# A gated-recurrence stage with one table for tanh and silu, an undecayed state, an out-projection over four heads and ScalarE work ordered by table set

## The chip, the cores and the metric

The kernel runs on the 8 NeuronCores of one Trainium2 chip, as two dies of four cores (0 to 3 and 4 to 7). Each core computes 2 of the 16 sequences and exchanges nothing with the others. The metric is the device time of the slowest core, in microseconds (us), as a median of runs. PE is the TensorE matmul engine, ACT is ScalarE, DVE is VectorE, POOL is GpSimd; PSUM is the memory that matmuls accumulate in.

Some runs here were in a slower state: one die (at times both) was granted a lower TensorE clock (0.927 against 0.975 in the profile of the four heads alone, below). Where stages are compared, I use a core whose die was undisturbed, and say which.

## The reference, cut to what matters

Two layers, each with a half-step SwiGLU FFN, a token mixer, cross-attention to 256 memory tokens and a second FFN. The mixer of layer 0 is HGRN2, a gated linear recurrence with 8 heads of 128 channels; that of layer 1 is a convolution module. D is 1024, 2048 tokens a sequence.

```python
def hgrn2_mixer(h, w_in, head_norm, w_out, lb):
    q, f, i, g = jnp.split(h @ w_in, 4, axis=-1)
    q = jax.nn.silu(q)
    log_forget = jnp.log(lb + (1.0 - lb) * jax.nn.sigmoid(f))
    k = (1.0 - lb) * jax.nn.sigmoid(-f)
    v = i
    # by chunks: G = cumsum(log_forget); o = (q exp(G)) @ state + masked scores @ v
    # new_state = state * exp(G_last) + (k exp(G_last - G))^T v
    ...
    o = rms_norm(o, head_norm)            # per head
    o = o * jax.nn.silu(g)
    return o @ w_out
```

## The kernel before: the parts that the change touches

All work is recorded as operations with their reads and writes. A list scheduler on the host then orders each engine's operations with assumed durations, and the engines run these fixed orders, with semaphores between them. So any edit gives a new order everywhere.

An HGRN stage has 32 *units* for each sequence: one head and 512 tokens. The unit's core, cut:

```python
bf, bq, bgt = grp(1), grp(0), grp(3)      # f, q, g: 8 matmuls of 128x512 each
act: A = Sigmoid(bf);  SQ = Sigmoid(bq);  SG = Sigmoid(bgt)
act: Bf = Ln(A * (1-lb) + lb)             # log of the forget gate
dve: SQ = bq * SQ;  gs = bgt * SG         # the two silus
pool: A = (1-lb) * (1 - A)                # k
dve: Cf = scan(rmask, Bf)                 # G, cumulated over 128 tokens
act: Bf = Exp(Cf);  Cf = Exp(-Cf)
pool: qg = SQ * Bf;  kg = A * Cf
...                                       # v projection (32 small matmuls), scores, k transposed
# state, four chunks of 128 tokens; e = Bf's last column of the chunk
for c in range(4):
    dve: dSe[c] = ds_psum[c] * e[c]
for c in range(4):
    dve: stF[c] = stF[c-1] * e[c] + dSe[c]        # float32 for the next step
    dve: stB[c] = stF[c-1] * e[c] + dSe[c]        # the same again in bf16, for the matmul
...                                       # o, its per-head norm with Ln and Exp
dve: og = o_psum * rsB;  ogT = og * head_norm * gs
# out-projection, for every head: 8 matmuls with a contraction of 128, 8 additions
for t4 in range(4):
    for half in range(2):
        pe: b = ogT[:, t4] @ w_out[head][:, half]
        dve: h[tt, half] += b
```

Elsewhere, norms take Sqrt on ACT and a reciprocal on DVE. The softmax denominators and the layer norm of the convolution stage take DVE reciprocals of 128x512. ACT takes its functions from table sets. Where an operation needs another set than the one before it, a table load stands in the trace (1.28 us each, 346 of them on core 4 before); the tool chain put it in wherever the order of ACT's operations asked for one.

The softmax here doesn't subtract the row's maximum and nothing guards it: scores larger than these inputs give would overflow.

## Time and profile before

The median was 6838.54 us in 3 runs (6781.57 to 7608.12). This is the view of the cores: span and mean granted clock.

```profile
core 0: 6843.2 us, clock 0.957
core 4: 6774.9 us, clock 0.966
die 0 (median of its cores): 6807.1 us, clock 0.963
die 1 (median of its cores): 6775.6 us, clock 0.966
```

Core 0 spent 314 us at 13/16 of the clock and core 4 none. I read core 4 from here on.

The windows view of core 4 before. Columns: stretch and its length, then for PE, weight loads, DVE, ACT and POOL the busy time (instructions), then granted clock, DMA share and GB/s. The rows are the first HGRN stage, the attention stage after it, the conv stage and the attention stage after that, each from its first matmul to that of the next stage.

```profile
571.00:1105.00 534.00, 386.24 (x2776) 214.87 (x2773) 415.45 (x839) 358.32 (x461) 133.40 (x127) 0.91 0.18 20
1105.00:1296.00 191.00, 171.42 (x899) 80.27 (x900) 144.89 (x174) 82.86 (x136) 12.17 (x14) 0.97 0.40 54
2253.00:2738.00 485.00, 420.96 (x1939) 186.91 (x1937) 335.16 (x270) 127.14 (x201) 209.18 (x67) 0.93 0.15 22
2738.00:2912.00 174.00, 158.34 (x842) 75.48 (x842) 115.13 (x115) 63.60 (x102) 5.98 (x7) 0.98 0.28 42
```

The groups of DVE in the HGRN window (busy us, mean ns of one, then idle time before and its releaser) show the additions to h and the doubled state update:

```profile
L555 DVE TENSOR_TENSOR h<-ps,h 128x512 f32<-128x512 f32 x232 | 143.0, 676 | 0.6 <-PE ps L1021 0.6
L988 DVE SCALAR_TENSOR_TENSOR arena<-arena 128x128 f32<-128x128 f32 x112 | 38.8, 347 | 0.0
L990 DVE SCALAR_TENSOR_TENSOR arena<-arena 128x128 bf16<-128x128 f32 x112 | 38.5, 344 | 0.0
```

The timeline of ACT on core 4 before, one unit of the steady part (start us, length us, instruction, idle time before and releaser):

```profile
873.53 1.28 ACT L930 ACT_TABLE_LOAD   x1 [0.93 <-DVE arena L990]
874.83 0.81 ACT L930 ACTIVATE arena<-arena,vecs 128x512 f32<-128x512 f32 x1
...
880.31 1.28 ACT L928 ACT_TABLE_LOAD   x1 [2.09 <-PE ps L921]
881.60 0.60 ACT L928 ACTIVATE arena<-ps 128x512 f32<-128x512 f32 x1
882.21 1.28 ACT L1005 ACT_TABLE_LOAD   x1
883.51 0.60 ACT L1005 ACTIVATE arena<-ps 128x512 f32<-128x512 f32 x1
884.20 0.63 ACT L1006 ACTIVATE arena<-arena 128x512 f32<-128x512 f32 x1
884.85 1.28 ACT L929 ACT_TABLE_LOAD   x1
```

Four loads stand in one unit: the order goes from Ln and Exp to one sigmoid, back for the per-head norm's Ln and Exp, and to a sigmoid again. The waits of PE in the same HGRN window (us in total, times, longest us) name both the DVE additions and ACT:

```profile
PE ps L1021 <- DVE h L555: 36.0, 41, 1.3
PE ps L943 <- ACT arena L1005: 33.1, 20, 1.7
PE ps L980 <- ACT arena L975: 30.5, 24, 5.9
```

### The profile page before, as it was taken

To read this page: it belongs to the slowest core of one execution; us is meant where nothing else is said; L and a number is where in the kernel's file an instruction comes from. 1 tells how busy PE (TensorE), PEld (TensorE's weight loads), DVE (VectorE), ACT (ScalarE), POOL (GpSimd) and SP (SyncE) were. 2 spreads that over 40 slices of the span, in tenths; PEclk is the share of its full clock that TensorE was granted. 3 is DMA by queue.
4 is the path that set the end of the run, shared out by engine and by line. 5 is a ranking of instruction groups with operands and counts; after the bars stand their busy time and mean duration, and the time that the engine had idled before them with its cause. 6 is when DMAs were issued, how large, how long until landed. Compare 5 with 4: busy or idle time off the path is not lost.

```text
span 6843.2 us, 92702 instructions; the slowest of 8 cores (6762.6 to 6843.2 us)
## 1 busy us (share of the span) xinstructions
PE 6095.5 (89%) x30572; PEld 2877.5 (42%) x31144; DVE 4501.0 (66%) x6622; ACT 1990.2 (29%) x2973; POOL 952.1 (14%) x717
## 2 busy tenths in 40 slices
PE   4998767999999987999889986689999999878998
PEld 2444334444444433444334443344444444334443
DVE  3658777756665487665656687776665563876656
ACT  2116665311311322311221266642112122223212
POOL 0002221000000453000000022200000004530000
PEclk9999999999999998999989989999998998989999
DMA  5222113322221201232432212134333312013221
GB/s 106 38 33 29 18 18 54 45 40 38 41 38 19 35 1 26 43 50 38 96 74 38 30 21 21 15 50 56 38 38 38 38 13 34 1 27 42 41 38 59
DMA packets 367914, 258.86 MB, mean 38 GB/s; under 512 B 114241, under 2 KB 331329, under 8 KB 367456
## 3 DMA queue, kind: packets, MB, share of 16 engines
q0 software_dynamic: 346560, 205.55, 23.6%
q1 hardware_dynamic: 20896, 47.35, 2.3%
q8 instruction: 270, 4.42, 0.3%
q14 instruction: 188, 1.54, 0.1%
HBM read 441.61 MB, written 16.78 MB: 67 GB/s over the span
## 4 chain that ended last, share of the span: by engine, by line
PE 76%; DVE 10%; issue 6%; ACT 5%; DMA 2%; SPq 1%; POOL 0%; DVEq 0%; ACTq 0%; POOLq 0%
PE ps L591 36%; PE ps L606 17%; PE ps L843 4%; PE ps L789 4%; PE ps L692 3%; PE ps L921 3%; PE ps L679 3%; PE ps L807 2%; PE ps L524 1%; DVE h L555 1%; DMA arena<-xattn_wkv 1%; DVE arena L819 1%; ACT L1005 1%; DVE arena L827 1%; SPq L470 1%
## 5 line engine op out<-in xcount | busy, mean ns | idle before, releaser
L591 PE MATMUL ps<-arena 128*128 128x512 bf16 x11037 | 2503.8, 382 | 21.9 <-ACT arena L593 7.8
L608 DVE SCALAR_TENSOR_TENSOR h<-ps,h 128x512 f32<-128x512 f32 x2816 | 1730.3, 682 | 7.6 <-PE ps L606 5.9
L591 PEld LDWEIGHTS ps<-arena 128*128 128x128 bf16 x11264 | 1105.2, 98 | 1347.3 <-issue 81.1
L594 DVE TENSOR_TENSOR arena<-ps,arena 128x512 bf16<-128x512 f32 x704 | 485.9, 691 | 1363.3 <-PE ps L591 1334.2
L606 PE MATMUL ps<-arena 128*128 128x512 bf16 x5505 | 1281.4, 382 | 16.1 <-DVE h L608 7.8
L593 ACT ACTIVATE arena<-ps 128x512 bf16<-128x512 f32 x704 | 419.9, 597 | 2970.7 <-PE ps L591 2963.2
L606 PEld LDWEIGHTS ps<-arena 128*128 128x128 bf16 x5632 | 551.0, 98 | 681.8 <-issue 51.7
L555 DVE TENSOR_TENSOR h<-ps,h 128x512 f32<-128x512 f32 x704 | 447.3, 682 | 159.4 <-PE ps L692 103.9
L552 POOL DMA_DIRECT2D arena<-ffn_w_in x176 | 156.5, 891 | 2593.2 <-PE ps L591 2004.3
L843 PE MATMUL ps<-arena 128*128 128x512 bf16 x1942 | 466.6, 397 | 46.4 <-DVE arena L819 30.7
L921 PE MATMUL ps<-arena 128*128 128x512 bf16 x1478 | 382.3, 406 | 14.2 <-ACT arena L975 4.0
L496 ACT ACTIVATE junk<-h 128x1024 bf16<-128x1024 f32 x288 | 302.1, 1050 | 300.6 <-DVE h L555 185.4
L817 POOL TENSOR_TENSOR arena<-identf,dwT 128x2688 bf16<-128x2688 f32 x64 | 315.0, 4923 | 370.7 <-PE ps L843 278.5
L520 DVE SCALAR_TENSOR_TENSOR hn_tok<-h,stat,gB 128x1024 bf16<-128x1024 f32 x256 | 322.4, 1276 | 41.4 <-PE ps L524 27.6
L843 PEld LDWEIGHTS ps<-arena 128*128 128x128 bf16 x1984 | 198.7, 101 | 304.8 <-issue 96.4
L1021 PE MATMUL ps<-arena 128*128 128x512 bf16 x506 | 157.5, 395 | 141.4 <-DVE h L555 75.6
L819 DVE TENSOR_TENSOR arena<-identf,dwT 128x1280 bf16<-128x1280 f32 x64 | 255.7, 3995 | 7.8 <-PE ps L789 4.8
L679 PE MATMUL ps<-arena 128*128 128x512 bf16 x994 | 235.1, 388 | 15.2 <-DVE arena L715 6.1
L789 PE MATMUL ps<-arena 128*128 128x512 bf16 x1002 | 243.8, 406 | 3.7 <-DVE arena L530 2.1
L715 DVE RECIPROCAL arena<-ps 128x512 f32<-128x512 f32 x64 | 211.4, 3332 | 39.9 <-PE ps L713 39.9
L524 PE MATMUL ps<-ident,hn_tok 128*128 128x128 bf16 x2048 | 160.1, 229 | 83.0 <-DVE hn_tok L520 62.3
L921 PEld LDWEIGHTS ps<-arena 128*128 128x128 bf16 x1536 | 153.2, 104 | 189.1 <-issue 55.1
(145 smaller groups left out, 4922.0 us busy)
## 6 DMA issues: line engine op xcount, KB each, us to landing
arena<-ffn_w_in POOLq DMA_DIRECT2D x176, 512.0 KB, 7.5
arena<-ffn_w_out POOLq DMA_DIRECT2D x88, 512.0 KB, 5.3
h<-x SPq DMA_DIRECT2D x8, 2048.0 KB, 15.1
arena<-hgrn_w_in POOLq DMA_DIRECT2D x64, 256.0 KB, 4.9
arena<-xattn_wkv POOLq DMA_DIRECT2D x16, 1024.0 KB, 12.4
y<-arena SPq DMA_DIRECT2D x32, 512.0 KB, 2.7
arena<-xattn_wq POOLq DMA_DIRECT2D x8, 1024.0 KB, 8.4
arena<-xattn_wo POOLq DMA_DIRECT2D x8, 1024.0 KB, 9.4
```

Of the source, the lines that this page charges most:

```text
L520: P.op("dve", lambda e, tt=tt, s=s: e.scalar_tensor_tensor(out=hn_tok[:, s, :], in0=h[:, tt, :], scalar=stat[:, 2, tt:tt + 1], in1=gB[:, g ...
L555: P.op("dve", lambda e: e.tensor_tensor(out=h[:, tt, half * 512:(half + 1) * 512], in0=psb(b), in1=h[:, tt, half * 512:(half + 1) * 512], ...
L591: P.op("pe", lambda e, bb=bb, ga=ga, k=k, j=j: e.matmul(psb(bb), lhsT=wiv[:, ga, k, j * 128:(j + 1) * 128], rhs=hnT[:, k, blk * 512:(blk + ...
L593: P.op("act", lambda e, bg=bg, j=j: e.activation(out=sg[j].ap, in_=psb(bg), func=AF.Silu), reads=psk(bg), writes=sg[j].keys())
L594: P.op("dve", lambda e, bu=bu, j=j: e.tensor_tensor(out=actv[:, j, :], in0=psb(bu), in1=sg[j].ap, op=ALU.mult), reads=psk(bu) + sg[j].keys ...
L606: P.op("pe", lambda e, bo=bo, j=j, t4=t4, half=half: e.matmul(psb(bo), lhsT=actv[:, j, t4 * 128:(t4 + 1) * 128], rhs=wov[:, j, half * 512: ...
L608: P.op("dve", lambda e, bo=bo, tt=tt, half=half: e.scalar_tensor_tensor(out=h[:, tt, half * 512:(half + 1) * 512], in0=psb(bo), scalar=0.5 ...
L679: P.op("pe", lambda e, b=b, k=k, c=c: e.matmul(psb(b), lhsT=wqv[:, c // 4, k, (c % 4) * 128:(c % 4 + 1) * 128], rhs=hnT[:, k, blk * 512:(b ...
L789: P.op("pe", lambda e, bb=bb, a=a, k=k, v=v, blk=blk: e.matmul(psb(bb), lhsT=v[:, a, k, :], rhs=hnT[:, k, blk * 512:(blk + 1) * 512], star ...
L819: P.op("dve", lambda e: e.tensor_tensor(out=dgv[:, NP_:CW, :], in0=identf[:, None, :].to_broadcast([128, CW - NP_, 128]), in1=dwT[:, c, NP ...
L843: P.op("pe", lambda e, b=b, j=j, c=c, lo=lo, dgv=dgv: e.matmul(psb(b), lhsT=dgv[:, j, :], rhs=uTv[:, c, lo:lo + 512], start=(j == 0), stop ...
L921: P.op("pe", lambda e, bb=bb, a=a, k=k: e.matmul(psb(bb), lhsT=v[:, a, k, :], rhs=hnT[:, k, blk * 512:(blk + 1) * 512], start=(k == 0), st ...
```

## The change

The intent, in five parts:

1. **Out-projection over 4 heads.** The gated outputs of four heads are kept, and PE sums the four heads in PSUM before one addition to h: 2 additions a unit on average instead of 8, the same number of matmuls. They come in lumps, after every fourth head.
2. **ACT order by table set.** Each ACT operation carries its set. The scheduler takes a ready operation of the present set first, unless the oldest ready one of another set has waited 6 us; it may also wait 1.3 us for one of the present set. Loads are written explicitly.
3. **Tanh and silu from one set** in place of three sigmoids and two DVE products. The forget gate is written with tanh(-f/2), and the factor of k goes into an Exp's bias.
4. **Undecayed state.** W[c] = e[c-1] * W[c-1] + ds[c], read straight from PSUM, four DVE operations instead of twelve; POOL scales all four chunks to bf16 at once.
5. **No Sqrt, no DVE reciprocal.** Norm factors by a power on POOL; softmax and layer-norm factors by Ln and Exp on ACT.

Smaller edits came with these: k's product moved from POOL to DVE, the last norm product from DVE to POOL, and the operations of projection, recurrence and out-projection are recorded in another order, which the scheduler uses as priority.

```diff
+            switch = 0.0
+            if e == "act" and ready[e]:
+                cand = sorted(ready[e])
+                ok = [c for c in cand if nodes[c[1]]["tbl"] in (None, table)]
+                first = cand[0]
+                fit = ok[0] if ok else None
+                if fit is not None and fit != first and t - nodes[first[1]]["ready"] > self.TBL_AGE:
+                    fit = None
+                if fit is None:
+                    ...                      # wait for an operation of this set, or switch
 ...
-                P.op("act", ... func=AF.Sigmoid, of f, q and g ...)
+                P.op("act", ... TH = Tanh(-0.5 * f), SQ = Silu(q), gs = Silu(g), tbl=SILU)
 ...
-                    P.op("dve", ... dSe = ds * e ...)
-                    P.op("dve", ... stF = prev * e + dSe ...)
-                    P.op("dve", ... stB = prev * e + dSe ...)
+                    P.op("dve", ... W[c] = W[c-1] * egl[c-1] + ds[c] ...)
+                P.op("pool", ... Sb = W * egl ...)
 ...
+                        for q in range(HG):      # HG = 4
+                            P.op("pe", ... matmul(psb(b), lhsT=ogT[q][blk]..., rhs=wo[q]..., start=(q == 0), stop=(q == HG - 1)))
                         add_to_h(tt, half, b)
 ...
-                P.op("act", ... Sqrt ...); P.op("dve", ... reciprocal ...)
+                P.op("pool", ... pow -0.5 ...)   # norms;  ACT Ln, Exp for softmax and layer norm
```

## The prediction

> **What bounds the kernel now.** The windows view by stage (slowest core) shows TensorE 96-99% busy in every FFN stage, so little can be gained there. The two HGRN stages (570 to 1134 and 3932 to 4497 us, 565 us each) are different: PE 72%, DVE 79%, ACT 67%, POOL 24%, granted clock 0.92. In the timeline a unit (one head, 512 tokens; 32 units a stage) repeats every 16.4 us there. From the groups, a unit's DVE work is 8 adds to h x 0.68, 8 state updates x 0.35, 4 scalings x 0.34, scan 1.23, six PSUM passes x 0.69 and one of 0.82: about 15.2 us, so DVE is over 90% busy in the steady part. ACT has 6.3 us of work plus about 3.6 table loads x 1.28 us, about 11 us. PE needs 24 matmuls x 0.216 + 32 x 0.056 + 20 x 0.056 + 9 x 0.216, about 10.0 us at full clock. The PE waits list agrees: the out-projection waits for the h adds and sigmoid products, the state matmuls for ACT.
>
> **What the change does, per unit.** DVE: h adds fall from 8 to 2 on average (-4.1 us), the doubled state update and the scaling become four fused ops (-2.8), both sigmoid products go (-1.4), the last two norm products become one DVE and one POOL op (-0.8); k's product comes from POOL (+0.8). About 15.2 becomes 7 us. ACT: about the same 6.4 us, table loads 3.6 becoming about 2: 9 us. POOL: three two-input ops of about 1.3 us, a small copy, DMA issues: 4 becoming about 5 us. PE: unchanged 10.0 us.
>
> A table load costs 1.28 us in the trace and the next ACTIVATE starts 1.30 us after the load's start[...]. I use 1.3.
>
> **How much is critical.** DVE stops being the limit. PE and ACT become close limits, and out-projection is lumped: in 12 of 16 units PE has 8.3 us and ACT (9 us, with waits near 10.5 to 11) sets the pace; in 4 of 16 PE has 15.2 us and sets it. Average near 12 us. With two buffers a unit's chain from silu(g) to the gated output, about 20 us, allows a unit each 10 us or so, not clearly binding. Stage: 32 x 12.2 + 30 for start and tail = 420 us, 145 saved, 290 for both.
>
> Outside: softmax reciprocals (64 x 3.33 us DVE) become two ACT ops of 0.6 us. PE waits little for them: 3 to 5 us in each of four attention stages. In the conv stages the 3.35 us reciprocals delay DVE's diagonal building (PE waits 15.6 us for it) and the last normalization (19.8 us): about 6 us each. 53 table loads for Sqrt go, but mostly where PE is busy. POOL now computes the norm factors behind its DMA issues; that may return some. Net 25 us.
>
> **Prediction.** From a normal fast time of about 6800: 6490 us, range 6390 to 6610. Faster by over 2%: 0.95, within 2%: 0.04, slower: 0.01.
>
> **What would show it.** HGRN stages of about 420 us with PE near 95% and DVE below 55%; unit period 10 to 11 us, 15 to 16 where out-projection runs; about 64 table loads of each set per stage; attention stages 3 to 5 us shorter, FFN unchanged.
>
> **What would make it wrong.** The static ACT order may wait for a table's op and stall the chain (unit period 13 to 14, 60 us a stage lost); POOL's three ops sit in the chain behind DMA issues that wait; the busier PE may be granted a lower clock; or ACT overlaps better and the stage is PE-bound near 365 us.

## More of the kernel before

In HGRN no engine is full over the stage: DVE 78%, PE 72%, ACT 67%. Nor is one in its steady part. These are 16 units, 17.1 us each, with DVE busy 76%:

```profile
805.90:1078.90 273.00, 186.78 (x1360) 102.53 (x1360) 207.36 (x434) 179.18 (x225) 63.64 (x62) 0.95 0.17 18
```

## The result, and the profile after

The median after is 6318.59 us (4 runs, 6312.94 to 6320.64). The runs of before, with one more taken beside it, now have a median of 6860.17 us. The ratio of fast runs is 0.9277 (95% interval 0.921 to 0.9344); it is the mean time of one kernel's fast runs over that of the other's of the same rounds, so not quite the ratio of the medians. Executions in which one die ran at a lower clock are left out of the means. The result is correct and faster by over 2%, but it lies 71 us under the lower end of my range.

The view of the cores after, the dies:

```profile
die 0 (median of its cores): 6310.9 us, clock 0.980
die 1 (median of its cores): 6313.4 us, clock 0.980
```

No core of this profile was at 13/16. The windows view of core 4 after, the same four stages and columns as above:

```profile
573.00:907.00 334.00, 316.33 (x2698) 196.04 (x2738) 231.66 (x355) 266.30 (x395) 162.74 (x162) 0.99 0.30 34
907.00:1099.00 192.00, 174.43 (x935) 86.92 (x951) 95.08 (x129) 84.78 (x146) 22.27 (x28) 0.96 0.36 49
2054.00:2523.00 469.00, 415.45 (x1901) 186.74 (x1938) 324.18 (x262) 127.11 (x200) 217.94 (x79) 0.94 0.16 22
2523.00:2686.00 163.00, 155.03 (x849) 76.96 (x864) 77.33 (x103) 70.01 (x122) 10.87 (x14) 1.00 0.32 46
```

PE is now busy 95% of the HGRN stage and its clock there is 0.99, not 0.91. DVE's work fell from 415 to 232 us and ACT's from 358 to 266 us. The table loads of ACT in the HGRN window, the whole group:

```profile
L330 ACT ACT_TABLE_LOAD x50 | 64.2, 1283 | 0.9
```

Before, the same window had 120 loads. The timeline of ACT after shows two units side by side between two loads; the order has paired them:

```profile
804.93 1.28 ACT L330 ACT_TABLE_LOAD   x1
806.22 0.60 ACT L1004 ACTIVATE arena<-ps 128x512 f32<-128x512 f32 x1
806.72 0.80 ACT L959 ACTIVATE arena<-arena,vecs 128x512 f32<-128x512 f32 x1
807.42 0.62 ACT L1005 ACTIVATE arena<-arena 128x512 f32<-128x512 f32 x1
807.94 0.80 ACT L959 ACTIVATE arena<-arena,vecs 128x512 f32<-128x512 f32 x1
...
814.33 1.28 ACT L330 ACT_TABLE_LOAD   x1
```

L959 is the Ln of the forget gate, here for two units with one load. PE's waits in the HGRN window have shrunk to a few us (longest two):

```profile
PE ps L972 <- DVE arena L964: 5.4, 4, 2.2
PE ps L982 <- ACT arena L973: 1.7, 2, 1.4
```

Where the time went, on core 4 of both profiles, each stage from its first matmul to the next stage's, sums over both sequences:

| part | before, us | after, us | change |
|---|---|---|---|
| HGRN (2) | 1069.0 | 665.2 | -403.8 |
| conv (2) | 970.0 | 937.0 | -33.0 |
| attention (4) | 727.7 | 714.4 | -13.3 |
| FFN (8, in 5 stretches) | 3909.7 | 3904.7 | -5.0 |
| start | 98.5 | 97.5 | -1.0 |
| span of core 4 | 6774.9 | 6318.9 | -456.0 |

The slowest core before was 68 us longer than core 4, mostly the lower clock of cores 0 and 1 in that run and no property of the change: core 0 was at 13/16 for 314 us, by that ratio an estimated 59 us lost.

### The profile page after: what moved, and what is told of

It is laid out like the page before. It is cut to its first block, busy times and chain, and to the rows that moved or that the text cites. A ratio compares the mean times of both kernels' runs of the same rounds, so it can differ in the third digit from the quotient of the medians.

```text
span 6319.1 us, 91318 instructions; the slowest of 8 cores (6303.1 to 6319.1 us)
## 1 busy us (share of the span) xinstructions
PE 5931.6 (94%) x31128; PEld 2832.1 (45%) x31128; DVE 3879.6 (61%) x5452; ACT 1762.5 (28%) x2819; POOL 1100.1 (17%) x928
## 4 chain that ended last, share of the span: by engine, by line
PE 86%; DVE 5%; issue 3%; DMA 2%; ACT 2%; SPq 1%; POOL 1%; DVEq 0%; ACTq 0%; POOLq 0%
PE ps L622 38%; PE ps L637 19%; PE ps L875 5%; PE ps L944 4%; PE ps L723 3%; PE ps L821 3%; PE ps L710 3%; PE ps L839 2%; PE ps L1016 2%; PE ps L956 1%; DMA arena<-xattn_wkv 1%; PE ps L555 1%; DVE hn_tok L551 1%; SPq L501 1%; PE ps L736 1%
## 5 line engine op out<-in xcount | busy, mean ns | idle before, releaser
L622 PEld LDWEIGHTS ps<-arena 128*128 128x128 bf16 x11264 | 1100.7, 98 | 1329.0 <-issue 12.9
L637 PEld LDWEIGHTS ps<-arena 128*128 128x128 bf16 x5632 | 545.7, 98 | 675.8 <-issue 37.0
L586 DVE TENSOR_TENSOR h<-ps,h 128x512 f32<-128x512 f32 x320 | 215.6, 688 | 202.0 <-PE ps L723 124.3
L875 PEld LDWEIGHTS ps<-arena 128*128 128x128 bf16 x1984 | 196.4, 99 | 281.2 <-issue 58.6
L851 DVE TENSOR_TENSOR arena<-identf,dwT 128x1280 bf16<-128x1280 f32 x64 | 273.7, 4276 | 6.2 <-PE ps L821 4.1
L583 POOL DMA_DIRECT2D arena<-ffn_w_out x88 | 62.2, 707 | 1090.4 <-PE ps L637 945.4
L944 PEld LDWEIGHTS ps<-arena 128*128 128x128 bf16 x1536 | 144.4, 98 | 156.9 <-issue 7.1
## 6 DMA issues: line engine op xcount, KB each, us to landing
arena<-xattn_wkv POOLq DMA_DIRECT2D x16, 1024.0 KB, 11.9
```

The lines of the kernel that those rows point to most:

```text
L622: P.op("pe", lambda e, bb=bb, ga=ga, k=k, j=j: e.matmul(psb(bb), lhsT=wiv[:, ga, k, j * 128:(j + 1) * 128], rhs=hnT[:, k, blk * 512:(blk + ...
L637: P.op("pe", lambda e, bo=bo, j=j, t4=t4, half=half: e.matmul(psb(bo), lhsT=actv[:, j, t4 * 128:(t4 + 1) * 128], rhs=wov[:, j, half * 512: ...
L875: P.op("pe", lambda e, b=b, j=j, c=c, lo=lo, dgv=dgv: e.matmul(psb(b), lhsT=dgv[:, j, :], rhs=uTv[:, c, lo:lo + 512], start=(j == 0), stop ...
L944: P.op("pe", lambda e, bb=bb, a=a, k=k: e.matmul(psb(bb), lhsT=v[:, a, k, :], rhs=hnT[:, k, blk * 512:(blk + 1) * 512], start=(k == 0), st ...
```

## The experiments

Theories for the HGRN stage. **D**: DVE's 15 us a unit were the limit before, so lightening DVE is the gain. **L**: the chain through the table loads was the limit, so ordering is the gain. For the miss of my range: either ACT's need was smaller than I had it, or PE sets the pace alone. The table counts HGRN plus the attention stage after it, in the first sequence, since the order moves work across that boundary; a "stage" is counted to the next stage's first matmul. "Quiet" units are those without out-projection.

| kernel (core read) | HGRN + attention, us | loads in HGRN |
|---|---|---|
| before (4) | 725 | 120 |
| before + order (4) | 683 | 66 |
| before + 4 heads (1) | 595 | 109 |
| before + both (0) | 542 | 41 |
| after (4) | 526 | 50 |
| after, no order (4) | 615 | 147 |
| after, per head (4) | 571 | 62 |
| after, decayed state (0) | 563 | 58 |
| after, sigmoids (4) | 546 | 54 |
| after, Sqrt and reciprocals (4) | 527 | 52 |

### Order alone on the kernel before

```diff
+ scheduler's part of the change, the explicit loads (no longer in the assumed durations)
+ and tbl= on every ACT operation
```

> The kernel before plus only the ACT order by table set (explicit loads; nothing else changed). Theory D (the HGRN stage before was limited by DVE's 15.2 us a unit): table loads in a stage fall from 120 to 50-65, but start-to-start of the stages moves little: 534 us to 505-530 us, total 1-2% faster. Theory L (the limit was the chain through table loads, two of which stand in each unit of the chain of waits): about 2.6 us a unit go, stage about 450 us, total 2.5% faster or more.

The stage took 503 us, just under D's 505 to 530; DVE was busy 430 us of it and ACT only 288. 54 loads less, 69 us of ACT, bought 31 us of stage. L's 450 us is refuted for the kernel before: loads alone were not the limit. PE's granted clock in the stage fell from 0.91 to 0.86, which may have cost part of the gain; no run separates this.

### Four heads alone on the kernel before

```diff
-  out-projection and 8 additions for every head
+  gated outputs of 4 heads kept, matmuls summed over them, 8 additions for 4 heads
+  sigmoid products in bf16, one buffer shared, to make room
```

> The kernel before plus only the out-projection over 4 heads (8 additions to h a unit become 2 on average, DVE 15.2 to 11.1 us a unit; products of q and g with their sigmoids kept in bf16 to make room). Theory D: stage 534 to 400-430 us (ACT with 3.6 loads a unit, about 11 us, is then level with DVE), total 3 to 4% faster. Theory L: stage stays above 480 us.

The stage took 416 us (core 1; this is the undisturbed die). D's range is met: 192 additions of 0.68 us fewer are 131 us of DVE, and HGRN plus attention fell by 130. PE (339 of 415 us) and ACT (335, with 109 loads) are now the busiest and DVE has 317. In the kernel before, PE also waited 36.0 us of the stage for these additions, and in the kernel after for none; no run separates this from DVE's time.

### Both on the kernel before

> The kernel before with both the out-projection over 4 heads and the table order. Theory D: DVE 11.1, PE 10.4, ACT 8.5 us a unit: stage 370-390 us, so most of the 200 us gained by the whole change is here already. If the DVE work that is left (doubled decayed state, sigmoid products) still mattered much, stage above 420 us.

The stage took 357 us on core 0, the windows view:

```profile
572.00:928.00 356.00, 320.09 (x2695) 194.83 (x2737) 330.81 (x665) 252.50 (x386) 156.57 (x127) 0.99 0.28 32
```

It is below my 370 to 390, with DVE 93% busy. HGRN plus attention fell by 183 of the 199 us of the whole change. Alone, order gave 42 and lumps 130; 183 is 11 more than the sum, too little to show an interplay, since edits below move the stage by up to 20 us in ways that their work does not explain.

### After, without the order

```diff
-    TBL_AGE = 6000.0
+    TBL_AGE = -1.0
```

> The kernel after with the ACT order by table set taken away (the age limit at -1, so ACT takes its oldest ready operation whatever its table). If the order carries the stage to the PE limit: loads rise from 50 to 90-120 a stage, ACT work to 10-11 us a unit, stage 334 to 365-400 us, the length I predicted. If lighter DVE alone does: stage stays below 345 us.

The stage took 424 us, more than the range I gave, because 147 loads came back, more than the kernel before had. The windows of core 4: the whole stage, then the quiet units 2 to 14 and 20 to 30.

```profile
572.00:995.00 423.00, 345.58 (x2714) 201.21 (x2712) 219.30 (x347) 389.94 (x486) 151.03 (x160) 0.94 0.21 25
607.70:753.50 145.80, 111.21 (x892) 63.95 (x889) 68.62 (x108) 141.39 (x176) 56.88 (x60) 0.94 0.24 24
842.30:961.60 119.30, 90.89 (x718) 54.25 (x719) 53.88 (x94) 113.79 (x143) 41.71 (x45) 0.90 0.15 19
```

In quiet units ACT is busy 95 to 97% of the time and DVE under 50%. So lightening DVE by itself does not reach the result; with everything else of the change in place, the order is worth 89 us of 615, where it was worth 42 on the kernel before and 53 with the additions lumped (595 to 542).

### After, out-projection per head

```diff
-            HG = 4
+            HG = 1        # and three buffers of out-projection weights
```

> The kernel after with the out-projection per head again (8 additions to h a unit). DVE work in the stage rises by 192 x 0.68 = 131 us to about 362 us, over the 334 us that the stage takes now: if DVE becomes the limit, stage 375 to 395 us. If the matmuls' spreading (out-projection no longer in lumps) helps as much as the additions cost: stage below 345 us.

The stage took 385.5 us, with DVE 335.5 and PE 347 us busy: D's range, and 45 us worse with the attention stage counted. PE is the busier of the two here, so that DVE is the limit is argued and not shown.

### After, with the decayed state

```diff
-  W[c] = W[c-1] * egl[c-1] + ds[c];  POOL: Sb = W * egl
+  dSe[c] = ds[c] * egl[c];  W[c] = W[c-1] * egl[c] + dSe[c];  Sb[c] = the same again
```

> The kernel after with the decayed state written twice, as before (12 DVE operations of 0.35 us a unit in place of 4, the POOL scaling gone). DVE work rises by about 90 us to 320 us of 334: stage 340 to 352 us, which would be most of the 21 us between the kernel before with lumps and order (355) and the kernel after (334). If only the total matters and PE stays the limit: below 338 us.

The stage took 351.6 us, within the range; with attention, 35 us worse (core 0 of both).

### After, with sigmoids

```diff
-  SQ = Silu(q);  gs = Silu(g)                       (silu set, with tanh)
+  SQ = q * Sigmoid(q);  gs = g * Sigmoid(g) on DVE  (sigmoid set, with tanh)
```

> The kernel after with sigmoid for q and g and DVE products, all three from the sigmoid table (which has tanh too), so the number of tables is the same. DVE work rises by 44 us to 275 us of 334, loads stay near 50: stage 334 to 340 us, the shared table of tanh and silu itself is worth next to nothing. If it were the shared table that gives the gain: above 350 us.

The stage took 350 us, over the 340 that I expected, with 54 loads. Here too all three functions share one set (sigmoid_and_others; the result was correct), as the three sigmoids did in the kernel before, so this run tests silu against sigmoid and product and not the sharing. The two products, with the order that came with them, cost about 20 us a sequence, though DVE was busy only 273 of 350 us. Why is left open. The single undoings don't add up either: the kernel before with order and lumps still has the decayed state, the sigmoids and k's product on POOL, and yet is better (542) than two of these. A new edit gives a new static order, and differences of 20 us a sequence may come from that; no run shows it.

### After, with Sqrt and reciprocals

```diff
-  norms: POOL pow; softmax, layer norm: ACT Ln, Exp
+  norms: ACT Sqrt, DVE reciprocal; softmax, layer norm: DVE reciprocal
```

> The kernel after with Sqrt on ACT and DVE reciprocals back everywhere (norms, softmax, layer norm), the table order kept. Conv stages 469 to 480-485 us, attention stages after a conv stage 163 to 173 us, HGRN stages within 5 us: in all 40 to 60 us slower. If the reciprocals lie off the critical path: under 15 us.

The conv stages took 481 us and the attention stages after them 175 to 176, so part 5 is worth about 13 us in three of these four and 7 us in the last. HGRN plus attention did not change (527). Core 4's span was 6370.3 us, 51 longer: the expectation holds.

### Less work for PE

```diff
-                    for k in range(KC):           # v projection
+                    for k in range(KC // 2):      # wrong result on purpose
```

> Wrong result on purpose: the kernel after with the v projection summed over half the input channels, 16 small matmuls a unit fewer (16 x 0.056 = 0.9 us). If PE is the limit of the whole HGRN stage: stage 334 to 305-310 us. If ACT sets the pace in 12 of 16 units, as I predicted: only the other 4 gain, stage 325 us or more.

The result was wrong (relative error 0.42). Quiet units took 8.4 us against 8.9 on the same core, over half of the 0.9 us taken away, with PE at 91 to 95% and ACT at 87 to 88%. Over units 2 to 30, 260.0 us against 276.1, 16 us were gained for about 25 us of PE taken away. HGRN's own stretch fell to 316 and 321 us, but with attention the sum was 526 against 527.6 us (core 0 of both). The 18 us gained by the last unit were given back at the boundary: in the stretch from 875 to 1090 us, PE waited 17.8 us for the normalized tokens of the next stage, against 7.3 us before this edit. So in the units PE's work counts for most of the pace, and the stage's end has a chain of its own.

### More work for ACT

```diff
+                for _ in range(2):
+                    P.op("act", ... activation(out=XD, in_=kgt[u], func=AF.Copy) ...)
```

> The kernel after with two ACT copies more in each unit (2 x 0.59 us into a spare buffer, result unchanged). The quiet units (no out-projection) take 8.8 us now, PE 95% and ACT 84% busy. If PE alone sets their pace and ACT has slack: 8.8 to 9.0 us. If ACT and PE set it together: 9.3 to 10 us, with ACT over 92%, and the HGRN stage with the attention stage after it 527 to 540-555 us. Units with out-projection (13.4 us, PE 98%) stay within 0.4 us.

The windows of core 4, units 2 to 14, 14 to 20 and 20 to 30, cut at the same operation (the scan of G) as those of the kernel after below:

```profile
598.00:712.80 114.80, 106.58 (x969) 67.81 (x979) 73.22 (x115) 102.92 (x166) 67.77 (x66) 1.00 0.33 32
712.80:783.00 70.20, 69.62 (x519) 40.01 (x527) 50.66 (x80) 49.14 (x74) 28.69 (x31) 1.00 0.36 42
783.00:871.50 88.50, 85.13 (x764) 54.06 (x775) 57.30 (x92) 80.62 (x132) 43.53 (x45) 1.00 0.21 25
```

By this cut a quiet unit took 9.2 us against 8.8, but the stretch of the lumps took 70.2 us against 80.4: the new order only moved PE's work across the cut (969 matmuls in the first window against 879). All 28 units took 273.5 us, against 274.6 before this edit, with PE at the same 95.5%. So the copies cost these units nothing, and PE, not ACT, sets their pace. The probe is weaker than planned: the scheduler found an order with 42 loads in place of 50, so that ACT's busy time in the 28 units rose by 15 us and not by 31. HGRN plus attention rose by 5.6 us, outside these units. My figures for "together" (540 to 555 us, ACT over 92%, lumps unchanged) were missed.

### A weaker order

```diff
-    TBL_AGE = 6000.0
-    TBL_LOOK = 1300.0
+    TBL_AGE = 2000.0
+    TBL_LOOK = 0.0
```

> The kernel after with a weaker table order: an operation of the other table may be passed over for 2 us only (6 before), and ACT no longer waits for one of its own table. Loads per quiet unit rise from 1.4 to about 2 or 2.5 (4.5 without any order). My prediction took 2 loads and 10.5 to 11 us. If loads are the price: each costs about 1.3 us once ACT is full, so 9.0 to 9.6 us at 2 to 2.5 loads. If waiting for the right table is itself a cost: no slower than 8.8 us.

The quiet units 2 to 14 and 20 to 30 of core 4:

```profile
603.80:712.50 108.70, 103.10 (x921) 64.97 (x932) 65.87 (x111) 101.48 (x147) 68.58 (x62) 1.00 0.34 33
791.60:891.50 99.90, 89.05 (x795) 56.07 (x805) 54.63 (x89) 89.95 (x126) 46.64 (x44) 0.98 0.19 22
```

With 2.25 and 2.5 loads a quiet unit, quiet units took 9.1 and 10.0 us, 9.5 on average (108.7 + 99.9 us over 22 units), and ACT was 93 and 90% busy. The 28 units took 287.7 us against 274.6, and HGRN plus attention 538.5 against 525.8. So even with my 2 loads a unit, 10.5 to 11 us was too long: ACT runs over 90% busy when its order is laid out for it.

### All diagonals of the conv stage on one engine

The conv stage writes 31 diagonal matrices for each channel block, 21 on POOL and 10 on DVE. The groups of core 4 after: ten diagonals, 1280 elements, took 4.3 us on DVE on average, though the fastest of them took 1.47 us. Two counter-experiments:

```diff
-                NP_ = 21
+                NP_ = 31      # all on POOL   (the other kernel: 0, all on DVE)
```

> An attempt at a better version: in the conv stage all 31 diagonals are built on POOL (about 7.1 us a channel block at the present 1.8 ns an element) and none on DVE (4.3 us now, [...]a sign of two engines in each other's way). If DVE's share of the diagonals is what PE waits for: conv stage 469 to 440-455 us. If POOL at 7.1 us is too slow for a PE period of about 11 us: longer than 469 us.

> The counterpart: all 31 diagonals on DVE, none on POOL. If POOL and DVE slow each other down, DVE alone builds all 31 in about 4.3 us, the time it takes for 10 now, and the other DVE operations get faster: conv stage 440-465 us. If there is no such contention: about 13 us a channel block, conv stage above 550 us.

All on POOL made the conv stage longer, 502 to 504 us. All on DVE made it shorter, 440 to 442 us on core 0 and 442.5 on core 4. The groups, core 4 after and then with all on DVE:

```profile
L851 DVE TENSOR_TENSOR arena<-identf,dwT 128x1280 bf16<-128x1280 f32 x32 | 138.9, 4340 | 3.0 <-PE ps L821 2.1 <-PE ps L875 0.8
```

```profile
L849 DVE TENSOR_TENSOR arena<-identf,dwT 128x3968 bf16<-128x3968 f32 x32 | 137.1, 4284 | 11.4 <-PE ps L873 8.7 <-PE ps L821 2.2 <-DVE arena L827 0.2
```

Alone, DVE builds 31 diagonals in the time in which it built 10 beside POOL. POOL's share was not a help but the cause. The times of single operations in the kernel after (shortest, median, longest) show it too:

```profile
L851 DVE TENSOR_TENSOR arena<-identf,dwT x64: 1474/5397/6003, 2170.5 to 5579.2; 128x1280 bf16<-128x1280 f32 x64
```

The 11 of these 64 during which POOL's 4.7 us share stood still took 1.48 us; 47 ran mostly beside it and took 5.1 to 6.0 us, about the rest of POOL's operation and then 1.4 us of their own. So the median of all 64 is 5.40 us, against 1.48 with POOL's share quiet. What holds DVE up there was not shown.

### A better version

```diff
-  NP_ = 21;  POOL: qg = SQ * LF
+  NP_ = 0;   DVE:  qg = SQ * LF
```

> An attempt at a version better than both: the kernel after with all 31 diagonals of the conv stage on DVE (conv stage 469 to 441 us as already seen) and, in the HGRN stage, the product of q with its decay moved from POOL to DVE, because DVE's scan (1.39 us against 1.23) and k product (1.15 against about 0.7) look slowed by POOL. If so: scan near 1.25, k product near 0.8, HGRN with the next attention stage 527 to 515-525 us, total 6230 to 6255. If DVE's extra 0.7 us a unit costs more: total above 6260.

The k product fell from 1.17 to 0.80 us, as expected, but the scan rose from 1.41 to 1.52. HGRN plus attention fell to 513 us (525 with the diagonals alone), conv stays at 442 us. Core 4's span was 6226.7 us against 6318.9. The lowest time of a run was 6245.16 us, where the kernel before had 6783.13 on the same chip; in the profiled run die 0 was at a lower clock (0.974 against 0.984) and took 6310.53. With the diagonals alone, the lowest was 6258.58 us. Both lowest times are about 1% below every run of the kernel after, which was not run beside them; this rests on fast single runs and on the stage times.

## Why the prediction was right or wrong, point by point

- **What bounds the kernel before: right in what to relieve, wrong in how full it was.** Taking 131 us of additions off DVE shortened HGRN plus attention by 130, and order alone does little there (534 to 503). But DVE was not "over 90% busy in the steady part": it was busy 207.36 of 273 us there, 76%, or 13.0 us a unit and not 15.2. My sum of mean durations counted the overlap of neighbouring operations twice (about 0.08 us at a joint, 2.0 us a unit in the trace). With 17.1 us a unit no engine was full; the unit was a chain of waits through all three.
- **DVE's new work: right.** About 7 us a unit predicted; 231.66 us over 32 units is 7.2.
- **The out-projection in lumps: right in size.** In the window of units 14 to 20 below, four lumps at my 15.2 us and two quiet units at 8.3 would be 77 us; it took 80. DVE was to be below 55% busy in the stage and was 69%, because the stage is shorter than I said.
- **The failed step: "in 12 of 16 units PE has 8.3 us and ACT (9 us, with waits near 10.5 to 11) sets the pace".** PE's 8.3 us was right. ACT's term was too large, so the wrong engine set the pace: PE does. I had named this case among the risks ("ACT overlaps better and the stage is PE-bound near 365 us"). These are the windows of core 4 after, the quiet units 2 to 14, the units 14 to 20 with out-projection, and the quiet units 20 to 30:

```profile
599.80:703.60 103.80, 97.14 (x879) 62.10 (x890) 71.23 (x110) 86.89 (x131) 60.70 (x60) 1.00 0.35 32
703.60:784.00 80.40, 78.64 (x604) 45.71 (x612) 52.62 (x88) 53.42 (x78) 34.65 (x38) 1.00 0.38 40
784.00:874.40 90.40, 86.37 (x782) 54.88 (x791) 59.94 (x94) 77.26 (x116) 50.39 (x47) 1.00 0.21 25
```

  Over the 22 quiet units, a unit took 8.8 us, PE 8.3 and ACT 7.5 (86.89 + 77.26, by 22). My 9 us for ACT had two errors. I took 2 loads where the order needs 1.36 (30 loads in the 22 units): 0.8 us. And I added up mean durations, while ACT's operations overlap when they stand back to back: in the timeline after, L959 starts at 806.72, 0.50 us after an operation of 0.60 us. The 117 such joints in the 22 units overlap by 0.10 us (median), 0.6 us a unit in all. The largest error was the 1.5 to 2 us of waits: the weaker order shows ACT 90 to 93% busy with more than 2 loads a unit, at 9.5 us a unit, and the two copies more of ACT in each unit cost the 28 units nothing. My 420 us counted the stage to its last matmul (565 before); on that count it took 374 (573.1 to 947.0), 46 less, and 24 quiet units times about 1.9 us (10.75 less 8.83) are 46. That the two agree is partly luck: my 12.2 us a unit was rounded up from 11.9, 11 us a stage. For two sequences this is 92 of the 114 us that HGRN gained more than I said; the rest is the stage's end, which overlaps the attention stage more (40 us of it instead of 30).
- **The order as a gain: undersized.** I counted its loads (3.6 a unit becoming 2; it is 1.6 over the stage with it and 4.6 without), but wrote of the static order itself only as a risk. Counted to its last matmul, as my 420 us were, the stage takes 374 us with the order and 464 without.
- **Outside HGRN: mechanism right, conv undersized.** I said 6 us for each conv stage; it was 16.5, and undoing Sqrt and reciprocals gives 13 of it back. Attention gained 13 in all, of 12 to 20 predicted, but that is luck: I said 3 to 5 us for each of four stages, and it was 11 and 6 after the conv stages and none after HGRN.
- **The baseline.** I started from 6800 us. An undisturbed core of before has 6775, which is 25 us of the miss. Together: 25 + 114 (HGRN) + 27 (conv, attention, FFN and start: 52 against 25) is 166 of 171 us; the rest is rounding.
- **The clock: a risk named with the wrong sign.** I feared a lower clock for a busier PE. The profile before has stretches of both (core 0 at 13/16 for 160 us from 5153 us on, PE busy 159 of them), but HGRN's granted clock rose, from 0.91 to 0.99. Core 4 was never at 13/16. What it had was half clock, in stretches of 3.4 us or multiples of it (69 of its 70 before): 464 us before and 256 after. PE's idle time in HGRN fell with it, from 148 of 534 us to 18 of 334. What starts such a stretch was not shown: in HGRN before, 20 of the 21 stretches follow 3.4 us in which PE was 29 to 54% busy and never idle for more than 2.1 us; the last, at its end, follows 3.4 us without PE work.

What stays open: what binds the end of the stage and its overlap with attention; how much of the 20 us for the sigmoid products is the products and how much the order that came with them; and the true optimum of the order, since each edit moves it.

## What to carry to other kernels

When one change relieves two engines, try each part alone and both together: here lumped additions gave 130 us, table order 42, both 183 of 199, and the same order gave 89 once the rest was in place. Cost an engine that has a planned order by its busy time in the trace, overlaps included and without an allowance for waits, before you let it set the pace over an engine that is nearly full. If you cut a stage into windows of units, compare the sum of the windows as well, since a new order moves work across the cuts. Splitting elementwise work between DVE and POOL can cost more than it shares out (here DVE took 4.34 us for 10 diagonals beside POOL and 4.28 for all 31 alone): measure the operation with the other engine quiet.
